# VectorE held to program order through the expert choice and the gate scatters of a PEER block

## The chip, the cores and the metric

The kernel runs on one core of one Trainium2 chip. The metric is the device time of one execution in microseconds (us). Engines are named as in the profile: PE is TensorE's matmul, PEld its weight load, DVE is VectorE, ACT is ScalarE, POOL is GpSimd, SP is SyncE, which issues most transfers.

## The reference, cut to what matters

The block computes an RG-LRU branch, latent attention, their mix, and then a layer of 16,384 small experts (PEER). Only the last part matters here. For each of four chunks of 128 tokens and each of 8 heads, two lists of 128 key scores are cut to their 16 best, the sums of the two lists give candidates, of which 16 experts are chosen, and their gates are a softmax:

```python
def one_chunk(xt):
    q = (xt @ w_q).reshape(BLOCK, PEER_HEADS, PEER_QDIM)
    s1 = jnp.einsum('chd,nd->chn', q[..., :half], keys1)
    s2 = jnp.einsum('chd,nd->chn', q[..., half:], keys2)
    t1, i1 = lax.top_k(s1, PEER_TOPK)
    t2, i2 = lax.top_k(s2, PEER_TOPK)
    cand = (t1[..., :, None] + t2[..., None, :]).reshape(BLOCK, PEER_HEADS, -1)
    cidx = (i1[..., :, None] * PEER_NKEYS + i2[..., None, :]).reshape(BLOCK, PEER_HEADS, -1)
    ts, sel = lax.top_k(cand, PEER_TOPK)
    idx = jnp.take_along_axis(cidx, sel, axis=-1)
    g = jax.nn.softmax(ts, axis=-1)
    act = jax.nn.gelu(jnp.einsum('chkd,cd->chk', u[idx], xt))
    return jnp.einsum('chk,chkd->cd', g * act, v[idx])
```

## The kernel before, in words

The expert layer is done in two ways. One chunk of tokens (chunk 0) fetches the rows of its experts by index (lines 915 to 937). The other three chunks (in the order 1, 2, 3 of `ORDER`) are done **densely**: PE multiplies the tokens with all 128 tiles of expert rows `u`, ACT takes the gelu, DVE multiplies with a dense matrix of gates that is zero where an expert was not chosen, and PE multiplies that with the rows `v`.

Before the dense stage stands the stage that the change touches, lines 896 to 903. Generators make its work in small steps, and `interleave` deals the steps out evenly:

- `choose(i, c)` (line 757) picks the 16 experts of a chunk for all heads, on DVE but for one exponential. It adds up candidates (lines 767 to 782, tiles `work`, `cx`); for each of 8 heads it takes the 16 largest by five instructions, `max`, `max_index`, `match_replace`, `max`, `max_index` (lines 787 to 791), of which each needs the result of one before it; for four groups it turns places into expert numbers (lines 803 to 806, tiles `oh`, `efx`); last it makes the gates: a subtraction on DVE (809), an exponential on ACT (810), and a sum, a reciprocal and a product on DVE (812 to 814).
- `scatter(gi, val, ef)` (line 843) makes the dense gate matrix of a chunk. It begins with four DVE instructions on the expert numbers (846 to 850, tiles `ei`, `ff`), three PE transposes (852 to 854, `sct`) and three ACT copies (`blk`, `it`, `gt`). Then 16 rounds of 8 tokens follow: DVE compares (879 `hb`, 884 `hot`), ACT scales (888 `wj`, 8 instructions), PE multiplies the round before (869 `sc`, 8 matmuls), ACT copies the result (870 `stg`, 2 instructions). `hb`, `hot` and `wj` have two buffers each. After each fourth round SP writes 2 MB to memory (872 `gd`).
- `first_ahead(j0, j1)` (line 830) does the first dense product for 38 of the 128 expert tiles ahead of the dense stage. A **block** is one such tile: two weight pieces arrive by DMA, ACT casts each to its high part (155 `ut_h`), DVE subtracts for the low part (156 `ut_l`), PE does 24 matmuls of 128x384 (181 and 182 on `ut_h`, 183 on `ut_l`, tile `a`), ACT takes the gelu (820 `act`).

The first choice runs beside 7 blocks; then come three scatters, beside 9, 10 and 11 to 12 blocks, and beside each scatter the choice of the next chunk, so that the choice of chunk 0 lies in the third one. The place between two scatters is called a **seam** below; the first seam is that between the first choice and the first scatter.

What is written is not yet what an engine runs: a scheduler puts each engine's instructions into an order of its own, by readiness in its model. Only inside `with in_order(tc, DVE)` (class at line 69) each DVE instruction is tied to the DVE instruction that was written before it. Before the change that holds for the dense stage (line 989) alone.

Of the kernel before, what the change touches and what calls it, by code (L numbers as in the profile page):

```python
# [50 lines left out]
ORD = (mybir.EngineType.DVE,)  # L51
# [5 lines left out]
ORDER = (1, 2, 3, 0)  # L57
# [7 lines left out]
def r32(t):  # L65
    return t.bitcast(F32)
# [40 lines left out]
def interleave(*gens):  # L107

    items = [[g, n, 0] for g, n in gens if n]
    while items:  # L110
        it = min(items, key=lambda i: i[2] / i[1])
        try:
            it[2] += next(it[0]) or 1
        except StopIteration:
            items.remove(it)
# [3 lines left out]
def hybrid_block_kernel(ctx: ExitStack, tc, hT, x, win, wkr, vecs, wgate, wrnn, watt, wuq, wukv, wout,  # L119
# [30 lines left out]
    efx = [cp.tile([P, NS], F32, name=f"efx{c}") for c in range(4)]  # L150
    gate = [cp.tile([P, NS], F32, name=f"gate{c}") for c in range(4)]
# [301 lines left out]
    def mm2(name):  # L453
        return ps_ring("post", name)
# [302 lines left out]
    def choose(i, c):  # L757

        work = po_.tile([P, 2 * PH * NCAND], F32, tag="work", bufs=1, name=f"work{c}")
        tf = work[:, PH * NCAND:PH * NCAND + 2 * P].rearrange("p (h a k) -> p h a k", h=PH, a=2)  # L760
        V.tensor_copy(tf, ti[i])
        V.tensor_scalar(tf[:, :, 0, :], tf[:, :, 0, :], float(P), None, op0=OP.mult)
        cd = work[:, :PH * NCAND].rearrange("p (h n) -> p h n", h=PH)
        cx = po_.tile([P, PH, NCAND], F32, tag="cx", bufs=1, name=f"cx{c}")

        def outer(dst, src, a0, na, b0, nb):
            V.tensor_add(dst.rearrange("p h (a b) -> p h a b", b=nb),
                         src[:, :, 0, a0:a0 + na].unsqueeze(3).to_broadcast([P, PH, na, nb]),
                         src[:, :, 1, b0:b0 + nb].unsqueeze(2).to_broadcast([P, PH, na, nb]))

        p0 = 0
        for a0, na, nb in ((0, 1, 16), (1, 1, 8), (2, 1, 5), (3, 1, 4), (4, 1, 3), (5, 3, 2), (8, 8, 1)):
            outer(cd[:, :, p0:p0 + na * nb], tv[i], a0, na, 0, nb)
            p0 += na * nb
            if a0 == 2:
                yield
        yield
        p0 = 0
        for grp in PAIRS:
            for a0, na, b0, nb in grp:  # L780
                outer(cx[:, :, p0:p0 + na * nb], tf, a0, na, b0, nb)
                p0 += na * nb
        yield
        ts = po_.tile([P, PH, TOPK], F32, tag="ts", bufs=1, name=f"ts{c}")
        sel = po_.tile([P, PH, TOPK], U32, tag="sel", bufs=1, name=f"sel{c}")
        for h in range(PH):
            V.max(ts[:, h, 0:8], cd[:, h, :])
            V.max_index(sel[:, h, 0:8], ts[:, h, 0:8], cd[:, h, :])
            V.match_replace(out=cd[:, h, :], in_to_replace=ts[:, h, 0:8], in_values=cd[:, h, :], imm_value=NEG)
            V.max(ts[:, h, 8:16], cd[:, h, :])  # L790
            V.max_index(sel[:, h, 8:16], ts[:, h, 8:16], cd[:, h, :])
            if h % 2:
                yield
        sf = po_.tile([P, PH, TOPK], BF16, tag="sf", bufs=1, name=f"sf{c}")
        V.tensor_copy(sf, sel)
        ef = efx[c].rearrange("p (h k) -> p h k", h=PH)
        n = 0
        for g, grp in enumerate(PAIRS):
            n += sum(na * nb for a0, na, b0, nb in grp)
            ks = slice(4 * g, 4 * g + 4)  # L800
            oh = po_.tile([P, PH, 4, NCAND], F32, tag="oh", bufs=1, name=f"oh{c}_{g}")[:, :, :, :n]
            ob = work.bitcast(BF16)[:, :PH * n * 4].rearrange("p (h n k) -> p h n k", h=PH, k=4)
            V.tensor_tensor(ob, sf[:, :, ks].unsqueeze(2).to_broadcast([P, PH, n, 4]),
                            cand_pos[:, :n].unsqueeze(1).to_broadcast([P, PH, n, 4]), op=OP.is_equal)
            V.tensor_mul(oh, ob.rearrange("p h n k -> p h k n"), cx[:, :, :n].unsqueeze(2).to_broadcast([P, PH, 4, n]))
            V.reduce_sum(ef[:, :, ks], oh, axis=AX.X)
            yield
        gw = gate[c].rearrange("p (h k) -> p h k", h=PH)
        V.tensor_sub(gw, ts, ts[:, :, 0:1].to_broadcast([P, PH, TOPK]))
        A.activation(gate[c], gate[c], AF.Exp)  # L810
        zs = po_.tile([P, PH], F32, tag="zs", bufs=2, name=f"zs{c}")
        V.reduce_sum(zs, gw, axis=AX.X)
        V.reciprocal(zs, zs)
        V.tensor_mul(gw, gw, zs.unsqueeze(2).to_broadcast([P, PH, TOPK]))
        yield
# [27 lines left out]
    def scatter(gi, val, ef):  # L843

        ei = sp_.tile([P, 2, NS], I32, tag="ei", bufs=1, name=f"ei{gi}")
        V.tensor_copy(ei[:, 0, :], ef)
        V.tensor_scalar(ei[:, 1, :], ei[:, 0, :], P - 1, None, op0=OP.bitwise_and)
        V.tensor_scalar(ei[:, 0, :], ei[:, 0, :], 7, None, op0=OP.logical_shift_right)
        ff = sp_.tile([P, 2, NS], F32, tag="ff", bufs=1, name=f"ff{gi}")
        V.tensor_copy(ff, ei)  # L850
        o = mm2(f"sct{gi}")
        TE.transpose(o[:, 0:P], ff[:, 0, :], ident)
        TE.transpose(o[:, P:2 * P], ff[:, 1, :], ident)
        TE.transpose(o[:, 2 * P:3 * P], val, ident)
        blk = sp_.tile([P, P], BF16, tag="blk", bufs=1, name=f"blk{gi}")
        A.copy(blk, o[:, 0:P])
        it = sp_.tile([P, P], F32, tag="it", bufs=1, name=f"it{gi}")
        A.copy(it, o[:, P:2 * P])
        gt_ = sp_.tile([P, P], F32, tag="gt", bufs=1, name=f"gt{gi}")
        A.copy(gt_, o[:, 2 * P:3 * P])  # L860
        yield

        def products(t0, hot, wj, stg):

            q, t8 = divmod(t0, TS)
            for h in range(0, SG, 4):
                o = ps.tile([P, 512], F32, tag="s", bufs=3, name=f"sc{gi}_{t0 + h}") if h else mm2(f"sc{gi}_{t0}")
                for u in range(4):
                    TE.matmul(o[:, u * P:(u + 1) * P], hot[:, h + u, :], wj[:, h + u, :], start=True, stop=True)  # L869
                A.copy(stg[:, :, t8 + h:t8 + h + 4], o.rearrange("p (t j) -> p j t", t=4))  # L870
            if t8 + SG == TS:
                nc.sync.dma_start(gd[gi, q], stg)

        last = None
        for t0 in range(0, P, SG):
            if t0 % TS == 0:
                stg = sp_.tile([P, NJ, TS], F32, tag="stg", bufs=1, name=f"stg{gi}_{t0 // TS}")
            hb = sp_.tile([P, SG // 4, P, 4], BF16, tag="hb", bufs=2, name=f"hb{gi}_{t0}")
            V.tensor_tensor(hb, iota4.unsqueeze(1).to_broadcast([P, SG // 4, P, 4]),
                            blk[:, t0:t0 + SG].rearrange("p (h t) -> p h t", t=4).unsqueeze(2)  # L880
                            .to_broadcast([P, SG // 4, P, 4]), op=OP.is_equal)

            hot = r32(vp.tile([P, D], F32R, tag="vh", bufs=2, name=f"hot{gi}_{t0}")).rearrange("p (t e) -> p t e", t=SG)
            V.tensor_tensor(hot, iota.unsqueeze(1).to_broadcast([P, SG, P]),  # L884
                            it[:, t0:t0 + SG].unsqueeze(2).to_broadcast([P, SG, P]), op=OP.is_equal)
            wj = r32(vp.tile([P, D], F32R, tag="vl", bufs=2, name=f"wj{gi}_{t0}")).rearrange("p (t e) -> p t e", t=SG)
            for u in range(SG):
                A.activation(wj[:, u, :], hb[:, u // 4, :, u % 4], AF.Copy, scale=gt_[:, t0 + u:t0 + u + 1])
            yield
            if last:  # L890
                products(*last)
            last = (t0, hot, wj, stg)
            yield
        products(*last)

    ahead = [1 + (LAG - LT - 1) * n // 72 for n in (0, 0, 14, 32, 50, 72)]
    ga = [first_ahead(a, b) for a, b in zip(ahead, ahead[1:])]
    na_ = [b - a for a, b in zip(ahead, ahead[1:])]
    interleave((key_scores(), 17), (ga[0], na_[0]))
    interleave((choose(0, ORDER[0]), 11), (ga[1], na_[1]))  # L900
    for i in range(3):
        c = ORDER[i]
        interleave((scatter(i, gate[c], efx[c]), 33), (choose(i + 1, ORDER[i + 1]), 11), (ga[2 + i], na_[2 + i]))
    scx.close()
    postx.close()

# [189 lines left out]
```

## Time and profile before

| | us |
|---|---|
| median of 3 runs (lowest to highest) | 1863.95 (1859.53 to 1864.54) |
| the profiled execution | 1864.08 |
| its span, first to last instruction | 1862.3 |
| PE busy | 1811.8 (97%) |
| DVE busy | 1444.0 (78%) |
| ACT busy | 968.5 (52%) |
| POOL busy | 355.2 (19%) |

The span is what the trace shows; 1.8 us of the execution lie around it. Times of events count from the span's start. A busy PE need not be at its full rate: matmuls overlap, and their ends are modelled. So PE's work is counted below by its starts, how far apart two matmuls begin.

### The profile page before, as it was taken

Reading aid. Unit: us, or ns where it says so; the run is one execution under the profiler, and the core shown is the slowest. Engines: PE = TensorE matmul, PEld = TensorE weight load, DVE = VectorE, ACT = ScalarE, POOL = GpSimd, SP = SyncE. Lnnn points to the kernel's source line nnn. Section 1 sums busy time; section 2 is a strip of 40 time slices with the busy share of each in tenths; the row PEclk is TensorE's granted clock in tenths of the full one; section 3 lists DMA queues with packets and bytes.
Section 4 is the critical chain, followed back from the end, with each engine's and each line's share of the span. In section 5 each row is a group of like instructions: output and inputs, shape, how many; then the busy total and the mean of one; then the engine's idle time right before and its main releaser. Section 6 shows DMA issues by size and latency. Waiting matters only on the chain.

```text
span 1862.3 us, 28323 instructions
## 1 busy us (share of the span) xinstructions
PE 1811.8 (97%) x9731; PEld 1601.3 (86%) x9731; DVE 1444.0 (78%) x3088; ACT 968.5 (52%) x2011; POOL 355.2 (19%) x295
## 2 busy tenths in 40 slices
PE   8999999999899999999999999999999999999997
PEld 7888778877778889998999999999999999997886
DVE  7787677777546999997558788877888878887775
ACT  6778576766333337999953333433333333333343
POOL 0100000000100000000014344434444443543310
PEclk9999999999999999999999999999999999999999
DMA  5333212112743223445589999998998989988764
GB/s 163 96 98 105 74 55 66 57 60 75 237 131 125 80 85 125 177 164 193 191 295 336 324 322 352 318 315 307 321 332 310 322 310 322 333 300 272 266 219 153
DMA packets 181600, 390.32 MB, mean 210 GB/s; under 512 B 16593, under 2 KB 68305, under 8 KB 179921
## 3 DMA queue, kind: packets, MB, share of 16 engines
q1 hardware_dynamic: 141632, 245.97, 39.0%
q0 software_dynamic: 39536, 142.00, 22.1%
q8 instruction: 76, 1.25, 0.3%
q10 hardware_dynamic: 288, 0.56, 0.1%
q14 instruction: 68, 0.55, 0.1%
HBM read 353.44 MB, written 34.08 MB: 208 GB/s over the span
## 4 chain that ended last, share of the span: by engine, by line
PE 30%; issue 16%; POOL 6%; DMA 5%; DVE 4%; ACT 1%; DVEq 0%; POOLq 0%; ACTq 0%
PE y L183 5%; PE y L181 5%; PE y L182 5%; PE a L183 4%; POOL v L915 4%; PE a L181 4%; PE a L182 4%; PE sc L869 4%; DMA v<-in_peer_v_dram,eidx 3%; POOL u L915 2%; DMA u<-in_peer_u_dram,eidx 1%; DVE hot L884 1%; DMA gt<-gd 1%; DMA ut_w<-in_peer_uT_dram 0%; DVE ut_l L156 0%
## 5 line engine op out<-in xcount | busy, mean ns | idle before, releaser
L183 PE MATMUL a<-xdh,ut_l 128*128 128x384 f32 x1024 | 347.4, 339 | 9.2 <-DVE ut_l L156 9.2
L181 PE MATMUL a<-xdh,ut_h 128*128 128x384 f32 x1024 | 348.6, 340 | 1.7 <-ACT ut_h L155 1.4
L182 PE MATMUL a<-xdl,ut_h 128*128 128x384 f32 x1024 | 345.5, 337 | 0.3 <-DVE xdl L156 0.3
L155 ACT CAST ut_h<-ut_w 128x512 fp32r<-128x512 f32 x256 | 157.8, 624 | 327.2 <-DMA ut_w<-in_peer_uT_dram 277.9
L181 PE MATMUL y<-vh,ch 128*128 128x512 f32 x768 | 299.6, 390 | 5.4 <-ACT ch L155 5.4
L183 PE MATMUL y<-vh,cl 128*128 128x512 f32 x768 | 301.6, 393 | 0.0
L182 PE MATMUL y<-vl,ch 128*128 128x512 f32 x768 | 301.0, 392 | 0.0
L915 POOL DMA_INDIRECT u<-in_peer_u_dram,eidx x128 | 161.4, 1261 | 666.3 <-DMA gt<-gd 441.4
L915 POOL DMA_INDIRECT v<-in_peer_v_dram,eidx x128 | 175.4, 1370 | 266.8 <-DVE acc L935 239.7
L156 DVE TENSOR_TENSOR ut_l<-ut_w,ut_h 128x512 fp32r<-128x512 f32 x256 | 169.5, 686 | 54.5 <-ACT ut_h L155 51.3
L183 PEld LDWEIGHTS a<-xdh,ut_l 128*128 128x128 f32 x1024 | 194.1, 190 | 11.4 <-DVE ut_l L156 11.0
L181 PEld LDWEIGHTS a<-xdh,ut_h 128*128 128x128 f32 x1024 | 194.3, 190 | 6.1 <-ACT ut_h L155 2.3
L182 PEld LDWEIGHTS a<-xdl,ut_h 128*128 128x128 f32 x1024 | 194.1, 190 | 3.9 <-DVE xdl L156 0.5
L156 DVE TENSOR_TENSOR vl<-vr,vh 128x1024 fp32r<-128x1024 f32 x128 | 157.6, 1232 | 42.9 <-ACT vh L155 41.9
L155 ACT CAST ch<-gt 128x384 fp32r<-128x384 f32 x128 | 65.7, 513 | 232.4 <-DVE gt L965 227.7
L181 PEld LDWEIGHTS y<-vh,ch 128*128 128x128 f32 x768 | 144.7, 188 | 34.8 <-ACT ch L155 6.5
L935 DVE SCALAR_TENSOR_TENSOR acc<-v,coef,acc 128x1024 f32<-128x1024 f32 x128 | 164.1, 1282 | 10.5 <-DMA v<-in_peer_v_dram,eidx 8.5
L183 PEld LDWEIGHTS y<-vh,cl 128*128 128x128 f32 x768 | 144.4, 188 | 31.1 <-DVE cl L156 0.8
L182 PEld LDWEIGHTS y<-vl,ch 128*128 128x128 f32 x768 | 144.5, 188 | 28.5
L926 DVE SCALAR_TENSOR_TENSOR jk<-u,xn 128x1024 bf16<-128x1024 f32 x128 | 156.6, 1223 | 13.7 <-DMA u<-in_peer_u_dram,eidx 11.3
L155 ACT CAST vh<-vr 128x1024 fp32r<-128x1024 f32 x128 | 133.8, 1045 | 32.5 <-PE y L183 28.5
L156 DVE TENSOR_TENSOR cl<-gt,ch 128x384 fp32r<-128x384 f32 x128 | 71.5, 559 | 81.8 <-ACT ch L155 81.8
(348 smaller groups left out, 3470.2 us busy)
## 6 DMA issues: line engine op xcount, KB each, us to landing
ut_w<-in_peer_uT_dram SPq DMA_DIRECT2D x256, 256.0 KB, 6.1
vr<-in_peer_v_dram SPq DMA_DIRECT2D x128, 512.0 KB, 6.7
gd<-stg SPq DMA_DIRECT2D x12, 2048.0 KB, 7.3
gt<-gd SPq DMA_DIRECT2D x96, 256.0 KB, 6.8
wq_w<-in_wq_dram SPq DMA_DIRECT2D x32, 256.0 KB, 2.8
wxr_w<-in_win_dram SPq DMA_DIRECT2D x16, 256.0 KB, 2.8
wgr_w<-in_win_dram SPq DMA_DIRECT2D x16, 256.0 KB, 2.7
wga_w<-in_win_dram SPq DMA_DIRECT2D x16, 256.0 KB, 2.7
```

The lines of the kernel that those rows point to most:

```text
L155: A.copy(dst_hi, src)
L156: V.tensor_sub(dst_lo, src, r32(dst_hi))
L181: TE.matmul(o, lh, rh, start=first, stop=False)
L182: TE.matmul(o, lh, rl, start=False, stop=False)
L183: TE.matmul(o, ll, rh, start=False, stop=last)
L869: TE.matmul(o[:, u * P:(u + 1) * P], hot[:, h + u, :], wj[:, h + u, :], start=True, stop=True)
L884: V.tensor_tensor(hot, iota.unsqueeze(1).to_broadcast([P, SG, P]), it[:, t0:t0 + SG].unsqueeze(2).to_broadcast([P, SG, P]), op=OP.is_equal)
L915: G.indirect_dma_start(out=t, out_offset=None, in_=src, in_offset=bass.IndirectOffsetOnAxis(ap=eidx[:, s:s + 1], axis=0))
L926: V.scalar_tensor_tensor(jk, t, 1.0, xn2, op0=OP.mult, op1=OP.mult, accum_out=coef[:, s:s + 1])
L935: V.scalar_tensor_tensor(acc, t, coef[:, s:s + 1], acc, op0=OP.mult, op1=OP.add)
```

## The change

The first choice and the three scatters, with the choices and blocks beside them, are put inside the same `in_order` that the dense stage has. No operation is added or taken away.

```diff
-    interleave((choose(0, ORDER[0]), 11), (ga[1], na_[1]))
-    for i in range(3):
-        c = ORDER[i]
-        interleave((scatter(i, gate[c], efx[c]), 33), (choose(i + 1, ORDER[i + 1]), 11), (ga[2 + i], na_[2 + i]))
+    with in_order(tc, *ORD):
+        interleave((choose(0, ORDER[0]), 11), (ga[1], na_[1]))
+        for i in range(3):
+            c = ORDER[i]
+            interleave((scatter(i, gate[c], efx[c]), 33), (choose(i + 1, ORDER[i + 1]), 11), (ga[2 + i], na_[2 + i]))
```

Lines after it move down by one. In the following lists of instructions `ut28_l0` is the first low piece of block 28, `hot1_120` the last round of the scatter numbered 1 (the second), `gate3` the gates of chunk 3; "x2" is two of a kind in a row.

DVE in the first choice, the search for the largest, before:

```order
L787 MAX ts1_7378<-work1_7269 128x8 x2
L788 MAX_INDEX sel1_7379<-ts1_7378,work1_7269 128x8 x2
L789 MATCH_REPLACE work1_7269<-ts1_7378,work1_7269 128x50 x2
L790 MAX ts1_7378<-work1_7269 128x8 x2
L791 MAX_INDEX sel1_7379<-ts1_7378,work1_7269 128x8 x2
```

The same place with the change:

```order
L787 MAX ts1_7378<-work1_7269 128x8
L788 MAX_INDEX sel1_7379<-ts1_7378,work1_7269 128x8
L789 MATCH_REPLACE work1_7269<-ts1_7378,work1_7269 128x50
L790 MAX ts1_7378<-work1_7269 128x8
L791 MAX_INDEX sel1_7379<-ts1_7378,work1_7269 128x8
L787 MAX ts1_7378<-work1_7269 128x8
L788 MAX_INDEX sel1_7379<-ts1_7378,work1_7269 128x8
L789 MATCH_REPLACE work1_7269<-ts1_7378,work1_7269 128x50
L790 MAX ts1_7378<-work1_7269 128x8
L791 MAX_INDEX sel1_7379<-ts1_7378,work1_7269 128x8
```

Two heads went side by side; now one head is finished before the next begins, so that each instruction stands right behind the one it needs. It is the same in all four choices.

DVE at the seam between the second and the third scatter, before:

```order
L879 TENSOR_TENSOR hb1_120_9378<-iota4_6199,blk1_8521 128x1024
L806 TENSOR_REDUCE efx0_80<-oh0_3_10324 128x8x4
L156 TENSOR_TENSOR ut27_l0_9326<-ut27_w0_9323,ut27_h0_9325 128x512
L884 TENSOR_TENSOR hot1_120_9380<-iota_73,it1_8523 128x1024
L812 TENSOR_REDUCE zs0_10407<-gate0_84 128x8
L813 RECIPROCAL zs0_10407<-zs0_10407 128x8
L814 TENSOR_TENSOR gate0_84<-gate0_84,zs0_10407 128x128
L156 TENSOR_TENSOR ut27_l512_9332<-ut27_w512_9329,ut27_h512_9331 128x512
L879 TENSOR_TENSOR hb2_0_9485<-iota4_6199,blk2_9432 128x1024
```

The same seam with the change:

```order
L884 TENSOR_TENSOR hot1_120_9380<-iota_73,it1_8523 128x1024
L809 TENSOR_TENSOR gate3_87<-ts3_8778 128x128
L812 TENSOR_REDUCE zs3_9418<-gate3_87 128x8
L813 RECIPROCAL zs3_9418<-zs3_9418 128x8
L814 TENSOR_TENSOR gate3_87<-gate3_87,zs3_9418 128x128
L846 CAST ei2_9422<-efx3_83 128x128
L847 TENSOR_SCALAR ei2_9422<-ei2_9422 128x128
L848 TENSOR_SCALAR ei2_9422<-ei2_9422 128x128
L850 CAST ff2_9426<-ei2_9422 128x256
L761 CAST work0_9438<-ti3_6194 128x256
L762 TENSOR_SCALAR work0_9438<-work0_9438 128x8x16
L767 TENSOR_TENSOR work0_9438<-tv3_6190 128x8x16
```

Before, the gates of chunk 3 and its `ei` and `ff` were made some 60 to 90 rows earlier, in the middle of the second scatter, and what stands at the seam is the end of the choice of chunk 0. With the change chunk 3's gates and numbers stand behind the last round of the second scatter; two more additions of line 767, two `ut28_l` and only then `hb2_0` and `hot2_0` follow.

PE at the same seam, before:

```order
L181 MATMUL a27_9457<-xdh_5359,ut27_h0_9325 128x384
L852 MATMUL sct2_9428<-ident_72,ff2_9426 128x128
L853 MATMUL sct2_9428<-ident_72,ff2_9426 128x128
L854 MATMUL sct2_9428<-ident_72,gate3_87 128x128
L182 MATMUL a27_9457<-xdl_5360,ut27_h0_9325 128x384
L183 MATMUL a27_9457<-xdh_5359,ut27_l0_9326 128x384
L869 MATMUL sc1_120_9403<-wj1_120_9382,hot1_120_9380 128x128 x2
L181 MATMUL a27_9457<-xdh_5359,ut27_h0_9325 128x384
```

With the change:

```order
L181 MATMUL a28_9510<-xdh_5359,ut28_h0_9447 128x384
L182 MATMUL a28_9510<-xdl_5360,ut28_h0_9447 128x384
L181 MATMUL a29_9591<-xdh_5359,ut29_h0_9500 128x384
L182 MATMUL a29_9591<-xdl_5360,ut29_h0_9500 128x384
L869 MATMUL sc1_120_9403<-wj1_120_9382,hot1_120_9380 128x128 x4
L869 MATMUL sc1_124_9409<-wj1_120_9382,hot1_120_9380 128x128 x4
L852 MATMUL sct2_9428<-ident_72,ff2_9426 128x128
L853 MATMUL sct2_9428<-ident_72,ff2_9426 128x128
L854 MATMUL sct2_9428<-ident_72,gate3_87 128x128
L183 MATMUL a28_9510<-xdh_5359,ut28_l0_9448 128x384
```

The transposes for the third scatter stood in the middle of block 27, whose matmuls lay between them and the products. Now block 27 is done by then, four matmuls of blocks 28 and 29 stand ahead, and the next ones need `ut28_l0`. The seam between the first two scatters is ordered likewise.

On ACT the exponential of a choice now stands behind the last `stg` copies of a scatter, at the third scatter too. On SP the load of `acc` (line 948) moves from the second scatter to behind the last write of `gd`, and one write of `gd` changes places with the load beside it; POOL's order is the same. Ahead of the first choice, the low pieces of block 2 move behind the last search in the key scores and the first five instructions of the choice.

## Rows read from the trace of the kernel before

**Rows 1.** Windows: length, busy us (instructions) of PE, PEld, DVE, ACT, POOL, PEclk, DMA, GB/s.
```profile
686.00:719.00 33.00, 29.49 (x154) 29.18 (x155) 31.64 (x144) 13.56 (x23) 0.00 (x0) 0.90 0.33 104
719.00:788.00 69.00, 67.35 (x475) 65.72 (x473) 68.78 (x254) 66.25 (x187) 0.00 (x0) 1.00 0.44 161
788.00:866.00 78.00, 71.63 (x476) 70.17 (x476) 73.28 (x182) 73.09 (x193) 0.00 (x0) 0.96 0.49 179
866.00:949.00 83.00, 81.75 (x565) 81.05 (x565) 45.37 (x57) 79.33 (x213) 0.00 (x0) 1.00 0.54 190
...
970.00:1700.00 730.00, 727.24 (x3656) 659.63 (x3655) 593.21 (x802) 263.61 (x434) 305.95 (x237) 1.00 0.93 320
```

**Rows 2.** Chain that ended last, handover to the dense stage: start us, us, what.
```profile
948.29 7.52 DMA gd<-stg
955.83 4.06 DMA gt<-gd
```

**Rows 3.** Groups by shape, PE, 719 to 949: count | busy us, mean ns | idle before.
```profile
L869 PE MATMUL sc<-wj,hot 128*128 128x128 f32 x768 | 93.0, 275 | 2.2 <-ACT wj L888 2.0
L181 PE MATMUL a<-xdh,ut_h 128*128 128x384 f32 x245 | 86.2, 352 | 1.4 <-ACT ut_h L155 1.4
L183 PE MATMUL a<-xdh,ut_l 128*128 128x384 f32 x245 | 84.7, 346 | 5.7 <-DVE ut_l L156 5.6
```

**Rows 4.** Timeline of PE: start us, us, instruction [idle before <-releaser].
```profile
688.88 0.69 PE L183 MATMUL a<-xdh,ut_l 128*128 128x384 f32 x1 [3.52 <-DVE ut_l L156]
...
718.74 0.33 PE L852 MATMUL sct<-ident,ff 128*128 128x128 f32 x1 [0.63 <-DVE ff L850]
...
793.75 0.69 PE L183 MATMUL a<-xdh,ut_l 128*128 128x384 f32 x1 [3.09 <-DVE ut_l L156]
794.24 0.52 PE L181 MATMUL a<-xdh,ut_h 128*128 128x384 f32 x1
794.56 0.52 PE L182 MATMUL a<-xdl,ut_h 128*128 128x384 f32 x1
...
931.18 0.34 PE L182 MATMUL a<-xdl,ut_h 128*128 128x384 f32 x1
...
935.16 3.73 PE L869 MATMUL sc<-wj,hot 128*128 128x128 f32 x32
938.65 0.42 PE L181 MATMUL a<-xdh,ut_h 128*128 128x384 f32 x1
```

**Rows 5.** Timeline of DVE, heads of a choice side by side, then places to numbers.
```profile
784.12 0.30 DVE L787 MAX8 ts<-work 128x8 f32<-128x50 f32 x2
...
784.43 0.20 DVE L788 FIND_INDEX8 sel<-ts,work 128x8 uint32<-128x50 f32 x1
...
785.70 0.31 DVE L787 MAX8 ts<-work 128x8 f32<-128x50 f32 x2
...
788.37 0.43 DVE L805 TENSOR_TENSOR oh<-work,cx 128x256 f32<-128x256 bf16 x1
788.83 0.42 DVE L806 TENSOR_REDUCE efx<-oh 128x32 f32<-128x256 f32 x1
```

**Rows 6.** Timeline of DVE, end of the first choice.
```profile
715.60 1.81 DVE L806 TENSOR_REDUCE efx<-oh 128x32 f32<-128x1600 f32 x1
...
718.41 0.28 DVE L850 CAST ff<-ei 128x256 f32<-128x256 int32 x1
...
718.72 1.28 DVE L156 TENSOR_TENSOR ut_l<-ut_w,ut_h 128x512 fp32r<-128x512 f32 x2
```

**Rows 7.** Timeline of ACT, end of the first scatter.
```profile
780.95 2.51 ACT L888 ACTIVATE wj<-hb,gt 128x128 f32<-128x128 bf16 x8
783.48 1.28 ACT L810 ACT_TABLE_LOAD   x1
784.77 0.31 ACT L810 ACTIVATE gate<-gate 128x128 f32<-128x128 f32 x1
784.99 3.99 ACT L870 COPY stg<-sc 128x512 f32<-128x512 f32 x8
```

## The prediction

> **What bounds the kernel now.** I first read the windows, to learn which engine sets the pace where. In the dense stage PE is busy for 727.24 of 730 us and the DMA engines at 0.93 [rows 1]: that stage has no slack, so whenever it starts later, the end comes later by the same amount. Then I read the chain of waits to see what lets it start: the last `gd` write (7.52 us) and the first `gt` load (4.06 us) follow directly on the last `stg` copy [rows 2]. So the change is worth what it does to the end of the third scatter, at 949 us, one to one.
>
> Between 719 and 949 us three engines are nearly full. PE is busy for 67.35, 71.63 and 81.75 of 69, 78 and 83 us, that is 9.3 us idle. ACT has 66.25 + 73.09 + 79.33 = 218.7 us of work in 230, 11.3 idle. DVE is full in the first two scatters (68.78 of 69, 73.28 of 78), but has only 45.37 of 83 in the third [rows 1]. This matters most for the forecast: nothing can be gained beyond ACT's 11.3 us, and whatever stops ACT and PE at a seam costs its full length, since neither can catch up.
>
> PE's own floor comes from its starts. From 931.18 to 935.16 lie 23 matmuls of 128x384, 0.173 us each; 32 `sc` take 935.16 to 938.65, 0.109 each [rows 4]. With 245 x 3 and 768 of them [rows 3] that is 127.2 + 83.7 = 211 us, in 230. Of the 19 us over, 9.3 are idle and some 3.1 are clock (0.96 over 78 us [rows 1]): 12.4 us of loss that can be placed. By wait these are 0.63 at the first seam, for `ff`; 3.09 at the second, for `ut_l` [rows 4], with about 1.5 of half clock behind it (after that wait two matmuls start 0.32 apart in place of 0.173 [rows 4]; I put half of the 3.1 here), 4.6 together; 1.25 in the third window [rows 1]; and the rest, 5.9, scattered.
>
> **The change part by part.** No instruction is added, so every term is one of order. PE, ACT and SP follow DVE. The sum is made against the profiled execution, 1864.08, which stands 0.1 above the median of 1863.95.
>
> *Start of the first choice.* PE waits 3.52 us for a `ut_l` already [rows 4]. The low piece of block 2 now stands behind the last search and the start of the choice, so some 10 fewer matmuls can run ahead of the wait (10 x 0.173 = 1.7); the list in front of it is shorter by about 0.7 us. I take **+1.0**, with 0 and 1.5 as ends.
>
> *Heads in a chain.* Two maxima that need nothing of each other take 0.30 us together where one instruction of this size takes 0.20, and two heads side by side take 784.12 to 785.70 = 1.58, or 0.79 a head. An instruction that needs its predecessor does not overlap it: 788.37 + 0.43 = 788.80, and the next starts at 788.83 [rows 5]. In a chain a head then takes five times 0.20 + 0.03, with some 0.07 for the values that the searches load, 1.22: +0.43 per head and +3.4 per choice. In the choices beside scatters this costs nothing as long as DVE has room; the cover is thin in the first two (0.2 and 4.7 us idle) and thick in the third (37.6) [rows 1]. In the first choice it is exposed.
>
> A rule speaks against this price. The Trainium skill's page "VectorE: DVE Perf Modes", section "The DRAIN you can't avoid", says that the next operation cannot start before the pipe is empty, whether or not a semaphore stands between. By that, a chain would cost nothing and the sum would be 3.4 lower. The overlap of two independent maxima in rows 5 disagrees.
>
> *First seam.* Before, the last `efx` ends at 717.41 and `ff`, four instructions later, at 718.69 [rows 6]: 1.28 us. Now the heads add 3.4 to the end of `efx`; about 0.8 of gate work moves from ahead of it to behind; and of the 1.36 us that DVE idles in the first choice (31.64 of 33 [rows 1]) between nothing and all is used up. So `efx` ends 1.2 to 2.6 later, 718.6 to 720.0. Then follow the subtraction, ACT's exponential (0.31 [rows 7]), three instructions for the gates and the 1.28 to `ff`: 2.5 us more, to 721.1 to 722.5. PE comes to `sct` at about 718.7, as before, and waits 2.4 to 3.8 where it waited 0.63; then again for `ut_l`, which stands behind five instructions of the next choice, but this overlaps the copies that ACT needs. With half clock behind such a wait I take **+4.5**, ends 2 and 5.8.
>
> *Second and third seam.* Before, PE had matmuls of a whole block between the transposes and the products, and the gates were ready. Now PE has four matmuls (0.7 us) while ACT scales the last round (2.51 [rows 7]): a wait of some 1.8 to 2. From the last products on all is one chain: a `stg` copy (eight take 3.99 [rows 7], so 0.5, and 0.1 of handing over), ACT's table load 1.28 and exponential 0.31 [rows 7], then seven small DVE instructions (the widest, `ff`, took 0.28 [rows 6]; 0.25 each gives 1.75), together 3.9. After 0.4 us of transposes PE waits for `ut_l`: five additions, 0.9 by the same pace, and one `ut_l`, 0.64 [rows 6], so some 1.1 is left. Idle: 2 + 3.9 + 1.1 = 7.0; with 1.5 of half clock, 8.5 a seam. This replaces 4.6 at the second and 1.25 at the third: 3.9 + 7.25 = **+11.2**. If DVE has the last round's `hot` done early and PE does not wait for it, and the table load runs ahead of the copy's end, a seam costs 4.5 (+3.2 in all); if the waits add up with a slow start of the next scatter's rounds, 10.5 (+15.2).
>
> *Between seams.* The scattered 5.9 us mostly stand in the second window, where DVE also did the next choice ahead of its turn and `ut_l` came late (5.6 of PE's waits in these groups name it [rows 3]). Dealt out evenly, DVE's work should no longer do that: **-5.0**, ends -5.9 and -2.
>
> *Handover.* The loads of `acc` and `gfb` come behind the last `gd` write; `acc`'s 512 KB are 1.6 us at 320 GB/s [rows 1]. They stand behind the write on which all waits, and the exponential of the last choice fits in the 11.6 us of write and load [rows 2]: **0**, ends 0 and 2.
>
> *The other three choices* add 3 x 3.4 us to DVE. Their cover is DVE's spare time, thin in two of three: 0 here, its failure is a rival below. **Sum**: 1.0 + 4.5 + 11.2 - 5.0 = 11.7, so **1875.8**, rounded to 1876.0. With all low ends it is 1863.4, with all high ones 1886.6. ACT gives a second estimate: its 218.7 us stay, each of two seams stops it by about 4.2 us (chain less its own copies, table load and exponential), former short waits stay at 4.5 to 11.3, so 232 to 238 us in place of 230, and the start adds 5: +7 to +13.
>
> **Rivals.** *The relief is worth more than the seams* (faster). Decided by whether the gates are ready when PE gets to the transposes: if the last choice step runs a round or two ahead of the scatter's end, DVE's order costs nothing at a seam, and of the 4.6 and the 5.9 us both go. The floor by ACT's 11.3 is 1853; half of 10.5 gives 1859, so about 1856. For it: DVE has room in the third scatter. Against: the lists put the exponential behind the last copies on ACT and the gates right ahead of `ff` at each seam.
>
> *No visible change.* Seams at their low end, +3.2, first seam +2, relief -5: +0.7, and 1865. For it: some of the chain may run beside the last products.
>
> *Starved rounds* (slower still). With DVE in order, a round's `hb` stands behind the places of the widest group: three instructions of about 1.8 [rows 6], 5.4 us, and DVE's own work for a round is 45.37/16 = 2.8 [rows 1]. Two buffers let ACT run for one round, 73.09/16 = 4.6, so a burst costs 5.4 + 2.8 - 4.6 = 3.6, three times 10.8: 1886.6. It decides once DVE's backlog exceeds a round. Against: the steps are dealt out evenly, and the last scatter's DVE is half empty.
>
> *Chains cost nothing.* A head takes 0.79 whatever stands beside it; then the first choice does not grow by 3.4 and the sum is 1872.4. This is what the Trainium skill's page "VectorE: DVE Perf Modes" ("The DRAIN you can't avoid") would make of it.
>
> **Numbers.** The forecast's case (seams on the path) has 0.50, no visible change 0.26, starved rounds 0.10, relief 0.09, free chains 0.05. What convinces me is the order at the seams; what I know least is the relief between them. A measurement tells 0.3%, 5.6 us, from no change: bounds 1858.5 and 1869.7. Faster by more is the relief, 0.09; within is no visible change, 0.26; slower are the other three, 0.65. The range, 1862.0 to 1887.0, reaches from just below the low ends of the sum to just above the starved rounds, and leaves out the relief and what exceeds these.
>
> **What would show it.** Right: in the changed profile PE waits 5 to 8 us in all at each of the second and third seams, first for `wj`, then at line 852 and 853 for `ff` and the gates, then at 183 for `ut_l`; ACT is idle there behind its exponential; matmuls after it start 0.32 apart; heads in the choices take about 1.2 us each; the last `gd` write starts about 12 us later, and the dense stage is as long as before. Wrong: if PE's idle time at these seams stays below 3 us, if DVE's `hb` and not the gates is what ACT waits for in most of the stage, or if the stage from 686 to 949 us gets no longer.

## The result, and the profile of the changed kernel

The change makes the kernel **slower**: 1892.06 us (median of 6 runs, 1888.82 to 1900.15) against 1861.63 (1859.53 to 1864.54), a ratio of 1.0165 with a 95% interval of 1.0150 to 1.0179, that is 30 us. The sign was forecast, the size was not: 1876.0 stood 12 us above the profiled execution before, and 1892 lies above the range.

The page of the changed kernel, its span and the busy times:

```profile
span 1890.1 us, 28339 instructions
PE 1820.4 (96%) x9731; PEld 1607.3 (85%) x9731; DVE 1458.2 (77%) x3088; ACT 969.0 (51%) x2011; POOL 356.2 (19%) x295
```

The span is 27.8 us longer, with as many instructions on each engine. The chain of waits at the handover answers to [rows 2]:

```profile
975.10 9.48 DMA gd<-stg
984.64 4.51 DMA gt<-gd
```

The last `gd` write starts at 975.10 in place of 948.29, 26.8 of the 27.8 us. So the loss lies ahead of the dense stage. (The write and the load themselves take 2.4 us longer, the way behind them 1.4 us less.) The windows of the changed kernel, cut at the transposes of each scatter, answer to [rows 1] (same columns):

```profile
686.00:728.00 42.00, 32.90 (x169) 31.36 (x169) 35.75 (x140) 13.03 (x23) 0.00 (x0) 0.92 0.26 88
728.00:811.00 83.00, 71.74 (x475) 69.17 (x475) 64.64 (x165) 71.22 (x193) 0.00 (x0) 0.95 0.41 149
811.00:892.50 81.50, 74.62 (x499) 72.99 (x500) 65.99 (x167) 72.80 (x196) 0.00 (x0) 0.96 0.44 158
892.50:976.00 83.50, 79.82 (x529) 78.64 (x530) 66.98 (x164) 74.16 (x198) 0.00 (x0) 0.96 0.49 176
989.00:1729.00 740.00, 737.02 (x3702) 668.47 (x3703) 600.94 (x814) 266.23 (x440) 310.84 (x240) 1.00 0.92 321
```

The dense stage is as full as before (737.02 of 740). In each of the three scatters PE, DVE and ACT are now all short of full at once: DVE idles 15 to 18 us, ACT 9 to 12, PE 4 to 11; before, DVE had idled 0.2 us in the first and PE 1.3 in the third. The instructions are the same, though DVE's take 10 us more in all (187.4 to 197.6 us busy; the heads, see below); for the rest, the engines wait for one another. The granted clock of PE is 0.95 to 0.96 in all three scatters; before it was 1.00 in two of them. It is low in one stretch behind each seam:

```profile
729.50:735.00 5.50, 5.50 (x17) 5.50 (x18) 5.04 (x10) 4.30 (x15) 0.00 (x0) 0.50 0.29 95
812.50:817.00 4.50, 4.50 (x14) 4.50 (x15) 4.50 (x10) 3.35 (x12) 0.00 (x0) 0.50 0.56 178
894.00:899.00 5.00, 5.00 (x16) 5.00 (x17) 2.81 (x4) 3.83 (x10) 0.00 (x0) 0.50 0.96 323
```

0.50 is the lower of the clock's two levels, 1.2 GHz. The 17, 14 and 16 matmuls there start 0.32 us apart in place of 0.173 [rows 4], so the three stretches cost some 2.5, 2.1 and 2.4 us.

Which waits these are, the view of waits tells (columns: who waits and for what, us in total, times, the longest). Before, 719 to 949 us:

```profile
DVE hb L879 <- ACT wj L888: 14.3, 11, 2.1
DVE ut_l L156 <- ACT ut_h L155: 12.7, 8, 3.0
DVE hot L884 <- PE sc L869: 8.0, 9, 1.9
...
ACT wj L888 <- DVE hb L879: 1.0, 2, 0.7
```

The changed kernel, 719 to 976 us:

```profile
DVE ut_l L156 <- ACT ut_h L155: 34.5, 16, 6.5
ACT wj L888 <- DVE hb L879: 14.2, 15, 3.1
...
PE sct L852 <- DVE ff L850: 10.5, 3, 4.3
DVE zs L812 <- ACT gate L810: 9.0, 3, 4.4
...
PE sc L869 <- DVE hot L884: 7.3, 7, 2.3
```

The lines on `ff` and on the gates are the seams, as forecast. Before, DVE was ahead: it waited 14.3 us at `hb` and 8.0 at `hot` for buffers that ACT and PE still read. In the changed kernel 0.5 us of that is left, and it is the compares that come late. The other three lines the forecast's sum had not priced: DVE stands for 34.5 us in front of low pieces whose high piece ACT has not cast, ACT stands for 14.2 us for `hb` (1.0 before), PE for 7.3 us for `hot`. One such place, on the timeline of DVE of the changed kernel in the first scatter (start us, us, instruction, idle before):

```profile
751.35 1.22 DVE L884 TENSOR_TENSOR hot<-iota,it 128x1024 f32<-128x1024 f32 x1
752.49 0.69 DVE L156 TENSOR_TENSOR ut_l<-ut_w,ut_h 128x512 fp32r<-128x512 f32 x1
754.60 0.69 DVE L156 TENSOR_TENSOR ut_l<-ut_w,ut_h 128x512 fp32r<-128x512 f32 x1 [1.42 <-ACT ut_h L155]
...
757.82 0.68 DVE L879 TENSOR_TENSOR hb<-iota,blk 128x1024 bf16<-128x1024 bf16 x1
```

and of ACT beside it:

```profile
751.53 2.52 ACT L888 ACTIVATE wj<-hb,gt 128x128 f32<-128x128 bf16 x8 [0.63 <-DVE hb L879]
753.95 0.61 ACT L155 CAST ut_h<-ut_w 128x512 fp32r<-128x512 f32 x1
...
758.59 1.61 ACT L888 ACTIVATE wj<-hb,gt 128x128 f32<-128x128 bf16 x5 [3.13 <-DVE hb L879]
```

ACT does a round of `wj` (751.53) before the cast (753.95). DVE cannot pass the `ut_l` that needs it and waits 1.42 us; then come two heads, each a chain; only then `hb`, at 757.82. ACT, with nothing to do since 755.45, takes up `wj` at 758.59, after 3.13 us. DVE waits for ACT, and so ACT waits for DVE. That DVE takes nothing out of turn agrees with the Trainium skill's page "PSUM — Partial Sum Buffer", section "Engine vs sequencer instructions", which calls the queues of ScalarE and VectorE strict FIFO; the rows show it at this `hb`, whose buffer was read last by the round of `wj` ahead of the one at 751.53.

### The profile page after: what moved, and what is told of

It reads as the page before. It is cut to its first block, busy times and chain, and to the rows that moved or that the text cites. A ratio compares the mean times of both kernels' runs of the same rounds, so it can differ in the third digit from the quotient of the medians.

```text
span 1890.1 us, 28339 instructions
## 1 busy us (share of the span) xinstructions
PE 1820.4 (96%) x9731; PEld 1607.3 (85%) x9731; DVE 1458.2 (77%) x3088; ACT 969.0 (51%) x2011; POOL 356.2 (19%) x295
## 3 DMA queue, kind: packets, MB, share of 16 engines
q8 instruction: 76, 1.25, 0.3%
## 4 chain that ended last, share of the span: by engine, by line
PE 78%; DVE 10%; ACT 6%; DMA 4%; issue 2%; DVEq 0%; ACTq 0%; SPq 0%
PE y L183 9%; PE y L182 9%; PE y L181 9%; PE a L183 8%; PE a L181 8%; PE a L182 8%; PE sc L869 3%; PE q L181 2%; PE q L182 2%; PE wgr_ps L228 2%; PE q L183 2%; PE wga_ps L228 2%; PE wgn_ps L228 2%; ACT wj L888 1%; DVE ut_l L156 1%
## 5 line engine op out<-in xcount | busy, mean ns | idle before, releaser
L183 PEld LDWEIGHTS a<-xdh,ut_l 128*128 128x128 f32 x1024 | 195.3, 191 | 12.4 <-DVE ut_l L156 12.4
```

The source lines that it names most:

```text
L183: TE.matmul(o, ll, rh, start=False, stop=last)
```

## The experiments

Ratios are to the kernel before on the same chip, with 95% intervals; in us, a ratio is taken times 1862. Two theories were set against each other: **H**, that DVE, standing at a `ut_l`, holds back the `hb` and `hot` behind it; and **S**, the forecast's own, that the seams make the loss.

### Which part of the change costs

Only the first choice in order:

```diff
     with in_order(tc, *ORD):
         interleave((choose(0, ORDER[0]), 11), (ga[1], na_[1]))
-        for i in range(3):
+    for i in range(3):
```

> Only the first choice is held to program order; the three scatters are free as before. In the changed kernel the first hb of the first scatter starts at 729.9 us against 719.9 before: 10 us later. Theory A (the first choice's part lies wholly on the path, the scatters have no slack to give it back): hb again near 730, then a stage of some 230 us as before, so about 1871 (+9 to +10 on before). Theory B (PE's matmuls of blocks are only put off, and the free scatters absorb part): 1863 to 1867.

Measured: 1.0052 (1.0032 to 1.0071), +10 us. As theory A; in its profile the first `hb` comes at 729.67 and the last write at 957.14, 8.9 us later than before.

Only the scatters in order:

```diff
-    with in_order(tc, *ORD):
-        interleave((choose(0, ORDER[0]), 11), (ga[1], na_[1]))
+    interleave((choose(0, ORDER[0]), 11), (ga[1], na_[1]))
+    with in_order(tc, *ORD):
         for i in range(3):
```

> Only the three scatters, with the choices and blocks beside them, are held to order; the first choice is free. From transposes of the first scatter to the last write of gd the changed kernel takes 247 us, before 230. Additive theory: +17 to +19, about 1880. If the two parts overlap (a late start hides some of the waits in the scatters, or the reverse): below 1876, or above 1884.

Measured: 1.0089 (1.0062 to 1.0116), 1878.41 us, +17. With the first, 26 of the change's 30 us; within the intervals the parts add.

### Which wait costs

The low pieces out of the chain. `in_order` gets a set of names to skip, `split` puts its subtraction into it:

```diff
         V.tensor_sub(dst_lo, src, r32(dst_hi))
+        free.add(nc.cur_bb.bb.instructions[-1].name)
...
-            if i.engine in self.engines:
+            if i.engine in self.engines and i.name not in self.free:
...
-    with in_order(tc, *ORD):
+    with in_order(tc, *ORD, free=free):
```

> All in order as in the change, but the low pieces of the blocks (ut_l, which wait for ACT's ut_h) are left out of the chain and may go wherever they are ready. Theory H (a blocked queue: DVE stands at ut_l until ACT has cast ut_h, 34.5 us in 16 waits, and the hb behind it come late, ACT waits 14.2 us for them, PE 9.3 us for hot and wj): ACT's waits for hb fall below 5 us and the time to 1876 to 1882. Theory S (the seams, that is the gates ready too late, make all of it): ACT's waits go elsewhere, the time stays within 3 us of 1892.

Measured: 1.0017 (0.9998 to 1.0037), +3 us. This one edit takes back 27 of the 30 us, more than H had promised. The view of waits, 719 to 953 us (lines of the code are 2 to 3 further down):

```profile
...
DVE zs L815 <- ACT gate L813: 7.8, 2, 4.5
DVE ut_l L158 <- ACT ut_h L157: 7.0, 8, 1.7
...
ACT wj L891 <- DVE hb L882: 5.2, 7, 1.2
```

34.5 and 14.2 us have become 7.0 and 5.2. The windows from the first `hb` to the last `gd` write: in the changed kernel,

```profile
729.93:975.10 245.17, 224.29 (x1495) 219.18 (x1495) 195.71 (x488) 216.67 (x584) 0.00 (x0) 0.96 0.45 163
```

with the low pieces free,

```profile
728.54:952.24 223.70, 212.91 (x1456) 207.49 (x1456) 192.91 (x485) 211.98 (x581) 0.00 (x0) 0.99 0.49 173
```

and before:

```profile
719.92:948.29 228.37, 219.10 (x1502) 215.44 (x1502) 186.51 (x491) 217.36 (x588) 0.00 (x0) 0.99 0.49 178
```

The stretch is 21.5 us shorter than in the changed kernel, and PE has its clock back (0.99). It is also 4.7 us shorter than before, but with 46 matmuls fewer, which PE did ahead, beside the first choice; at 228.37 / 1502 = 0.15 us each they are 7 us, so that is no gain. All other DVE instructions are still in program order, and the gates still stand at the seams: DVE waits 7.8 us for their exponential. But no wait of PE's matmuls for `ff` is left in the view (10.5 us in the changed kernel). So theory S falls as an account of the loss: here a seam costs only as long as PE has no other work, and the work it lacked were blocks whose low pieces stood behind the seam (behind the transposes PE waits for one, see the lines on the second seam below). With the order on DVE the scheduler also places ACT's and PE's instructions anew, in this run and in all that follow; no run changes DVE's order and nothing else.

The opposite release, `hb` and `hot` out of the chain:

```diff
             V.tensor_tensor(hb, iota4.unsqueeze(1).to_broadcast([P, SG // 4, P, 4]),
...
+            free.add(nc.cur_bb.bb.instructions[-1].name)
...
             V.tensor_tensor(hot, iota.unsqueeze(1).to_broadcast([P, SG, P]),
...
+            free.add(nc.cur_bb.bb.instructions[-1].name)
```

> The opposite release: the low pieces stay in the chain, but the two compares of each round, hb and hot, are left out of it. Theory H (what costs is the work behind a blocked ut_l): within the scatters the compares no longer stand behind it, ACT's waits for hb fall below 5 us, but the first choice stays as late as in the change (+9) and PE's own waits for ut_l stay; 1874 to 1880. Theory L (what costs is that the low pieces themselves come late, for PE): no gain from this release, 1888 to 1894.

Measured: 1.0076 (1.0054 to 1.0098), +14 us; 1878.16. Theory H: 16 us come back. The waits, 719 to 956 us:

```profile
DVE ut_l L158 <- ACT ut_h L157: 2.6, 3, 1.8
ACT wj L892 <- DVE hb L881: 2.5, 2, 1.5
```

Not only are ACT's waits for `hb` down to 2.5 us: DVE's waits for `ut_h` fell to 2.6 us although every low piece stands where it stood in the text. So the two were one ring, and opening it at either end shortens both waits. The window from first `hb` to last write:

```profile
728.23:955.10 226.87, 219.44 (x1502) 216.80 (x1502) 192.71 (x490) 215.48 (x585) 0.00 (x0) 0.98 0.48 178
```

That is 1.5 us less than before, with as many matmuls, so in this profile the scatters lose nothing in sum, though PE still waits 7.5 us for `ff` at the seams; the last write is 6.8 us late because the first `hb` is 8.3 late, as H expected. Against the other release, whose last write stands at 952.24, that explains 2.9 of the 11 us between the two times; the rest lies behind the last write and is not explained. More buffers for `hb`, `wj` or the pieces, another way to loosen the ring, were not tried.

The low pieces written a block later, right ahead of the matmuls that use them and no longer with the prefetch of their weights:

```diff
             w = nextw.pop(j, None) or wload(peer_uT[j], D, f"ut{j}")
+            flush()
             if j + 1 <= LAG - LT:
+                late[0] = True
                 nextw[j + 1] = wload(peer_uT[j + 1], D, f"ut{j + 1}")
+                late[0] = False
```

(`split` puts its subtraction on a list while `late` is set, `flush` issues the list.)

> All in order, but in the text the subtractions of a block stand one block later: right ahead of the block's own matmuls and no longer with the prefetch of its weights. Theory H: at that place ACT has long cast ut_h, DVE's 34.5 us of waits for it fall below 12, the hb come on time; 1870 to 1880. Rival: now PE waits for the low pieces, since they come directly ahead of their use; PE's waits for ut_l rise above 10 us and the time stays at 1885 to 1895.

Measured: 1.0148 (1.0125 to 1.0171), 1892.4 us: no gain that can be told from noise. H was wrong on the time here. Its waits fell (ACT's for `hb` to 7.8), but others came (719 to 978 us; `split` is at 157 and 165, PE's matmuls at 191 and 193, `hot` at 897):

```profile
DVE hot L897 <- PE sc L882: 18.2, 8, 5.9
DVE zs L822 <- ACT gate L820: 16.3, 4, 6.0
DVE ut_l L165 <- ACT ut_h L157: 12.4, 5, 4.1
...
PE a L191 <- ACT ut_h L157: 6.7, 2, 3.6
```

DVE's waits for `ut_h` are 12.4 in place of 34.5, as expected, but DVE now stands 18.2 us at `hot` until PE frees a buffer, where the changed kernel showed 0.5, and 16.3 us at the gates' exponential, where it showed 9.0. The rival's own number, PE's waits for low pieces above 10 us, held only with the first choice counted in (11.0 from 686 us on, 3.8 in the scatters); PE also waits 6.7 us for `ut_h`. Another place for `ut_l` only chose another wait. How these waits hang together in detail was not settled.

ACT in program order as well, so that its casts stand where DVE's subtractions expect them:

```diff
-    with in_order(tc, *ORD):
+    with in_order(tc, *ORD, mybir.EngineType.Activation):
         interleave((choose(0, ORDER[0]), 11), (ga[1], na_[1]))
```

> The change, and ACT held to program order over the same stretch as well, so that the casts ut_h stand on ACT where the subtractions ut_l that need them stand on DVE. Theory M (the waits come from two orders that do not fit: a fixed one on DVE, one by a model on ACT that puts ut_h behind later wj): DVE's 37.9 us of waits for ut_h fall below 20 and the time to 1872 to 1884. Theory R (a fixed order as such costs, since each wait for a buffer stops all that stands behind it): ACT's waits for PE's release of buffers grow, 1888 or more.

Measured: 1.0360 (1.0341 to 1.0380), 1929.03 us, 36 us worse than the change. Theory M falls. Theory R had the direction, but not the wait: ACT's waits for buffers that PE releases did not grow, the ring did, and a wait for a buffer that a DMA releases (719 to 1016 us):

```profile
DVE ut_l L156 <- ACT ut_h L155: 69.3, 31, 6.1
ACT wj L888 <- DVE hb L879: 31.5, 27, 4.8
...
ACT stg L870 <- DMA gd<-stg: 25.6, 9, 5.3
```

Both of the ring's waits have doubled, and ACT now also stands 25.6 us (1.0 with the change) at `stg` copies until the `gd` write before has read their buffer. Here two engines kept to the written order stood still for each other more often than one.

### The seams and the heads

The gates written ahead of the places:

```diff
+        gw = gate[c].rearrange("p (h k) -> p h k", h=PH)
+        V.tensor_sub(gw, ts, ts[:, :, 0:1].to_broadcast([P, PH, TOPK]))
+        A.activation(gate[c], gate[c], AF.Exp)
         sf = po_.tile([P, PH, TOPK], BF16, tag="sf", bufs=1, name=f"sf{c}")
...
             V.reduce_sum(ef[:, :, ks], oh, axis=AX.X)
+            if g == 1:
+                zs = po_.tile([P, PH], F32, tag="zs", bufs=2, name=f"zs{c}")
...
```

> All in order, but in the text of the choice the gates' subtraction and exponential stand ahead of the places' conversion, and sum, reciprocal and product behind the second of its four groups, so at a seam nothing waits for ACT's exponential. Theory S: PE's waits for ff (10.5 us in three) fall to some 2 to 4, with the half clock behind them about 10 to 12 us are saved, 1880 to 1882. Theory H: these waits shrink too, but the scatters stay slow between seams; 4 to 7 us are saved, 1885 to 1888.

Measured: 1.0132 (1.0097 to 1.0167), 1886.61 us, some 6 us off. That is H's number, but the interval overlaps the change's (1.0150 to 1.0179) and also holds the 10 to 12 of S, so the time does not decide; and in its profile the last write, at 974.0, is only 1.1 us earlier than with the change. The waits tell more. PE's waits for `ff` are down from 10.5 us to 0.7 and DVE's for the exponential are gone. But in the view of waits, 719 to 974 us, the ring has taken it up:

```profile
DVE ut_l L156 <- ACT ut_h L155: 42.8, 19, 5.9
...
ACT wj L889 <- DVE hb L880: 18.1, 16, 3.1
PE sc L870 <- DVE hot L885: 9.4, 8, 4.1
```

The heads written two side by side:

```diff
-        for h in range(PH):
-            V.max(ts[:, h, 0:8], cd[:, h, :])
...
+        for h0 in range(0, PH, 2):
+            hs = (h0, h0 + 1)
+            for h in hs:
+                V.max(ts[:, h, 0:8], cd[:, h, :])
+            for h in hs:
+                V.max_index(sel[:, h, 0:8], ts[:, h, 0:8], cd[:, h, :])
...
```

> All in order, low pieces in the chain; only the heads are written two side by side, so each instruction again has one between itself and the one it needs. Heads fall from 1.30 us to about 0.8, some 4 us a choice. Theory 1 (the chain costs in the first choice alone, as the prediction had it): 3 to 4 us off, about 1888. Theory 2 (the longer choices also hold hb back in the scatters): 6 to 12 off, 1880 to 1886. Theory 3 (DVE stands at ut_l for as much longer): no gain, 1891 to 1893.

Measured: 1.0121 (1.0101 to 1.0142), 1883.49 us, 8 us off: Theory 2, though by both intervals it may be anything from 3.5 to 13, so that the time does not quite exclude Theory 1. Its window from first `hb` to last write (245.17 us in the changed kernel):

```profile
726.64:969.00 242.36, 225.12 (x1493) 220.52 (x1493) 187.00 (x488) 217.58 (x585) 0.00 (x0) 0.96 0.46 164
```

In this profile 3.3 us come off ahead of the first `hb`, and 2.8 behind it. So the chained heads cost something in the scatters too, but less than their length: DVE has 8.7 us less to do there (195.71 to 187.00).

### The first choice, and a kernel faster than both

The scatters in order without the low pieces, the first choice free (the edits of the second and third experiment together):

> Only the scatters are in order, the first choice is free, and the low pieces are out of the chain. With the low pieces free and all else in order the first hb was still 8.6 us later than before, but from there to the last gd write it took 223.7 us in place of 228.4. Additive theory: without the late start, 1857 to 1860, faster than before by 3 to 6. Rival (the late start of the scatters was paid for by blocks done ahead, which shorten the scatters): 1863 to 1867, no better than before.

Measured: 0.9994 (0.9982 to 1.0006): no difference from before. The rival was right on the time. Its window from first `hb` to last write:

```profile
720.48:944.85 224.37, 214.91 (x1491) 210.51 (x1490) 194.02 (x487) 213.71 (x583) 0.00 (x0) 1.00 0.48 176
```

4.0 us less than before with 11 matmuls (1.7 us) fewer: in this profile order without the low pieces gains some 2 us in the scatters, too little for the whole time to tell.

The first choice in order without the low pieces, the scatters free (first and third together):

> Only the first choice is in order, and its low pieces are out of the chain. With them in the chain the ratio was 1.0052. Theory H for the first choice too (what delays PE there is that ut_l of the blocks stand behind the search): 1.000 to 1.001, 1862 to 1864. Theory C (the heads in a chain and the gates behind them, 8.6 us to the first hb, are on the path): 1.004 to 1.005, 1870 to 1872. The difference of the two kernels with free low pieces, with the first choice in order (1.0017) and without (0.9994), would let one expect 1.0023.

Measured: 1.0007 (0.9990 to 1.0025). Theory H again: of the 10 us that the first choice in order costs, 8 hang on the low pieces; the interval also holds the 1.0023 that its expectation derived from two other kernels. In this run's profile the window from first `hb` to last write is

```profile
724.92:952.11 227.19, 216.16 (x1470) 210.51 (x1469) 183.81 (x473) 215.63 (x586) 0.00 (x0) 0.99 0.48 176
```

The first `hb` comes 5.0 us later than before, the last write 3.8 later. Part of the late start is paid for by blocks that PE does meanwhile: 1470 matmuls are left in place of 1502.

Low pieces free, heads in pairs and gates early, all in order (three edits above together):

> All in order with the low pieces free, and in the text of the choice two heads go side by side and the gates stand ahead of the places. Heads should fall from 1.30 us to about 0.8, 4 us a choice; the chain to ff at the first seam loses the exponential, some 2 us. If these lie on the path: 5 to 6 us below the 1867 of the kernel with free low pieces alone, 1861 to 1862. If PE is covered by blocks there anyway: within 2 us of 1867.

Measured: 0.9984 (0.9960 to 1.0009), 1863.45 beside 1866.35: 6 us below free low pieces alone if the ratios are compared (by the intervals 0 to 12), but not to be told from before. The same with the first choice free, in 5 rounds:

> A try at a faster kernel: only the scatters in order, low pieces out of the chain, heads in pairs, gates early in the text; the first choice free. The scatters alone with free low pieces gave a ratio of 0.9994 to before, and pairs and early gates took a further 0.0033 off where all was in order. If these add: 0.996, about 1857. If the first choice, free, does its heads in pairs anyway and has nothing to gain: 0.998 to 1.000, no better than before.

Measured: 0.9983 (0.9970 to 0.9995), 1859.76 us beside 1862.64: 3 us faster than before and the only kernel of twelve here whose interval lies below 1, if only just. That is the second of the two expectations, 0.998 to 1.000. Its window from first `hb` to last write:

```profile
718.92:942.80 223.88, 215.54 (x1491) 211.08 (x1490) 186.79 (x489) 215.49 (x585) 0.00 (x0) 1.00 0.50 177
```

223.88 us in place of 228.37, at a clock of 1.00, with 11 matmuls fewer.

## Why the prediction was wrong in size

*Right.* The handover is one to one here: 26.8 us at the last write gave 27.8 at the end, with 2.4 us for the longer write and load, which the sum had at 0, made good behind them. Over all profiles the way from the last write to the end is 909 to 921 us, so the rule holds to some 6 us. The head in a chain, forecast at 1.22 us, takes 1.31; the timeline of DVE of the changed kernel, from one head to the next:

```profile
695.49 0.21 DVE L787 MAX8 ts<-work 128x8 f32<-128x50 f32 x1
...
696.80 0.19 DVE L787 MAX8 ts<-work 128x8 f32<-128x50 f32 x1
```

In pairs it is again 0.80, and 8 us come off: having the needed instruction right in front costs 0.5 us a head. The rival of the free chains falls. The rule of the Trainium skill's page "VectorE: DVE Perf Modes", section "The DRAIN you can't avoid", as the prediction took it, did not hold for these instructions; the same section adds that a next instruction that is not held starts earlier, and that agrees with the overlap in [rows 5].

*The start and the first seam*, forecast at 1.0 + 4.5 = 5.5: the first `hb` stands at 729.93 in place of 719.92, 10.0 later, and the half clock behind the seam adds 2.5, 12.5 in all; alone this part costs 10 us of time. The wait for the first `ut_l` grew from 3.52 to 4.88, as term and size had it. Under-sized was the rest: the heads' 0.5 in place of 0.43; the exponential, taken at 0.31, without the table load of 1.28 ahead of it, which ACT began only behind casts and a gelu, at 724.42 (DVE waits 1.27 us there); and 2.38 and 0.99 us in which DVE stood at low pieces inside the choice, where the sum had let DVE's idle time go down. With the low pieces free, 8 of the 10 us went.

*The second and third seam*, forecast at 7.0 us idle each: they are there in the forecast's order, but smaller. PE at the second, in the changed kernel:

```profile
804.63 2.16 PE L869 MATMUL sc<-wj,hot 128*128 128x128 f32 x16
811.05 0.45 PE L852 MATMUL sct<-ident,ff 128*128 128x128 f32 x1 [4.26 <-DVE ff L850]
...
812.47 0.69 PE L183 MATMUL a<-xdh,ut_l 128*128 128x384 f32 x1 [0.55 <-DVE ut_l L156]
812.96 0.52 PE L181 MATMUL a<-xdh,ut_h 128*128 128x384 f32 x1
813.28 0.52 PE L182 MATMUL a<-xdl,ut_h 128*128 128x384 f32 x1
```

4.26 + 0.55 = 4.8 us; no wait for `wj` stands ahead of the last products, 0.92 for a gelu does just ahead of this piece. The third has 3.9:

```profile
892.51 0.45 PE L852 MATMUL sct<-ident,ff 128*128 128x128 f32 x1 [3.37 <-DVE ff L850]
...
893.93 0.69 PE L183 MATMUL a<-xdh,ut_l 128*128 128x384 f32 x1 [0.55 <-DVE ut_l L156]
```

The matmuls behind start 0.32 apart, as forecast, but for longer: the slow stretch costs 2.1 and 2.4 us in place of 1.5.

*The step that failed* is "Between seams": "Dealt out evenly, DVE's work should no longer do that: **-5.0**". From first `hb` to last write the stretch grew by 16.8 us (228.4 to 245.2). Of these, 2.5 are the half clock behind the first seam, and the second and third seam, idle time and half clock, are (4.8 + 2.1 - 4.6) + (3.9 + 2.4 - 1.25) = 7.3 in place of 11.2. So what lies between them cost some 7 us instead of giving back 5: 12 of the 15 us by which the sum was too low. (Start and first seam were 7.0 too low, the other two seams 3.9 too high.) The 5 us were too much by the step's own rows as well: of the 5.6 us of PE's waits for `ut_l`, 3.09 are the wait at the second seam, which the sum had already replaced; 2.5 were left. And the step looked at how much DVE does, not at what each of its instructions waits for. Before, the scheduler's order did not keep `hb` behind low pieces that were not ready: DVE spent 12.7 us at low pieces and ACT's waits for `hb` were still 1.0. Held to the written order, late casts on ACT became late `hb`, and late `hb` late casts. The relief that the step named showed only once the low pieces were free, and then at some 2 us.

*The rivals.* "Starved rounds" had the place (`hb` late, ACT starved) and, at 1886.6, nearly the time, but the wrong cause: it counted bursts of the choice's widest group. Of the choice's own instructions the heads are part of it, 8 us by the pairs, 3 of them ahead of the first `hb`; the larger part is standing at `ut_l`, 27 us by the release (the two overlap). "What would show it wrong" named the line, `hb` and not the gates being what ACT waits for; that is what the waits show. The cover given to the other three choices, "thin in two of three", held in part: pairs took 8.7 us off DVE's work there and 2.8 off the stretch. The idle time of DVE held to order lies in front of a wait, and what stands behind that wait cannot use it.

## What to carry to other kernels

Before an engine is held to written order, list for each instruction which engine it waits for, and what stands behind it that this engine will need next: here a ring through two queues cost far more than the 2 us of shorter waits that the order saved. Leave those few instructions out of the chain that wait for another engine's side work; here that alone brought back 27 of 30 us. Idle time of an engine is cover for more work only if that work may be done in it.

## What the runs showed of the hardware that was not expected

Holding a second engine, ACT, to the written order made matters worse by 36 us, although its casts then kept to the same written order as DVE's subtractions. A first `hb` 8.6 us later put the last write only 4.0 us later where the low pieces were free and PE had blocks to do; with the low pieces in the chain (only the first choice in order), 9.8 later became 8.9. And freeing `hb` and `hot` alone cut DVE's waits for ACT's casts from 34.5 to 2.6 us, without moving a single low piece in the program's text.
